# A two-layer decoder trunk on one core: another place for the first tiles of weight chunks, and another order of steps in both mixers

## The chip, the core and the metric

The kernel runs on one core of a Trainium2 chip. Times are microseconds on the device for one execution of the whole program, and a comparison takes the median of several runs. The core has five engines that work side by side, each through its own list of instructions in order: TensorE (PE, with its weight loads shown as PEld), VectorE (DVE), ScalarE (ACT), GpSimd (POOL), and SyncE (SP), which here only issues transfers. They wait for each other by semaphores.

## The reference, cut to what matters

The input is 256 tokens of width 1,024 in float32. Two layers each do this, and a last RMSNorm follows:

```python
for layer in range(2):
    h = h + 0.5 * swiglu(rms_norm(h, ffn1_norm[layer]), w_gate, w_up, w_down)
    h = h + mixer(rms_norm(h, mix_norm[layer]))
    h = h + 0.5 * swiglu(rms_norm(h, ffn2_norm[layer]), w_gate, w_up, w_down)

def swiglu(x, w_gate, w_up, w_down):         # 1024 -> 2816 -> 1024
    return (silu(x @ w_gate) * (x @ w_up)) @ w_down
```

The mixer of layer 0 projects to q, k, v of eight heads of 64 and to u, v of a gating branch. The heads attend over three dilated windows, which the kernel folds into one additive mask. The branch takes gelu of u and v, normalises v, mixes it over positions with a causal 128 x 128 matrix for each of four groups, and multiplies by u. Both parts go through one output projection. The mixer of layer 1 is causal attention with 16 heads of 64; with 256 tokens its blocks come down to the one own block.

## The kernel before, in words

The residual stream is kept turned around in `X`: eight tiles of 128 columns of x by 256 tokens. For each matmul stage `Next` makes two tiles of it, `xTh` (x times the norm's gain, rounded to the short float32 format that TensorE takes) and `xTl` (what the rounding left). The weights are cut in the same way into `whi` and `wlo`. One product is then three matmuls (`mm3`, lines 199 to 202): whi with xTh (line 200), whi with xTl (line 201), wlo with xTh (line 202). The factor 1/rms of the norm is put in when a result is taken out of PSUM (`norm["row"]`, `norm["col"]`).

Weights come as a stream of chunks (`Stream`, line 40) of 2,048 columns per partition, 1 MB each. `load_one` has SP load a chunk into one of three raw buffers. `split_parts` makes whi on ACT (line 87) and wlo on DVE (line 88) out of it, in a few pieces (`cuts`), into one of four buffers each, which have 64 elements (`LINE`) to spare. `take` hands a chunk to PE; `free` gives its buffers back and has the next ones loaded and split. The order of chunks is written out in lines 161 to 182.

A chunk of a 256-wide weight block has eight tiles of 256 columns, one for each tile of x. PE goes through it twice, for the first 128 columns of each tile (j = 0) and for the second (j = 1): 2 x 8 x 3 = 48 matmuls, each with 128 weight columns against 256 columns of xTh or xTl. All tiles stand `SHIFT` = 16 elements past the start of the buffer, and the start is a multiple of 256 bytes, as are those of xTh, xTl and the other moving tiles. In some chunks, those with `reset`, the first two tiles, here called the head of the chunk, stand at 0 in place of 16 (`at`, line 78). In the feed-forward blocks these are the chunks named in `again`: 1 and 3 in the first block, 2 and 3 in the others. In the mixers they are the chunks of columns 1536 and 0 (first) and 0 and 512 (second).

A feed-forward block (`ffn`, line 429) makes 22 chunks of gate and up columns in turn (n = 0 to 21). `sums` and `spread` behind chunks 1 and 2 make the norm's factor; `gated` takes each pair out into hT. Then come the down columns: 12 chunks, 528 matmuls. In the last block the down product is made in rows of tokens instead (`finish`), so x is turned back for it by 16 transposes on PE and four copies on ACT (`turn_back`, line 440), behind chunk n = 2.

In the mixers one tile of 128 output columns after the other is made on PE (24 matmuls each, `tile_of`), and between these the steps of attention are hung in as events at numbered slots (`at`, `run_events`): `scores(h)` (two products for each half of the queries, softmax on DVE and ACT, scaling on ACT in the first mixer and on POOL in the second), `turn(h)` (three transposes and a split), `weighted(p)` (the product with v for two heads), and `mixing(g)` of the gating branch. `put_k` takes a k tile out of PSUM and has POOL copy halves of kh and kl to the other partitions (lines 625 and 626). A slot is one such tile, or one k step of the output projection (`project`): slots 12 to 19 in the first mixer, 20 to 27 in the second. In the first mixer the tiles come as u, u, q, k, q, k by chunk.

The first chunk of the program is special (`begin`, line 346): x comes in rows of tokens, and PE turns it by transposes (line 394), half before part 0 and half before part 2 of the chunk; ACT and DVE make xTh and xTl from PSUM between the pieces of the split. `heat` puts in matmuls without use.

Of the kernel before, what the change touches and what calls it, by code (L numbers as in the profile page):

```python
# [10 lines left out]
F32 = mybir.dt.float32  # L11
F32R = mybir.dt.float32r
# [3 lines left out]
S = 256  # L16
# [9 lines left out]
PATTERNS = ((128, 1), (512, 4), (2048, 16))  # L26

RAW, SPL = 3, 4
PAIRS = 3
HEAT0, HEAT1 = 6, 4  # L30


LINE, SHIFT = 64, 16
EDGE, GAP = 56, 32

RESET = 2
DOWN = ((0, 8), (8, 8), (16, 6))


class Stream:  # L40
# [7 lines left out]
    def add(self, src, nk, w, shift=0, cuts=(), reset=0):  # L48

        loads = 4 if not self.specs else 2 if len(self.specs) < 4 else 1  # L50
        cuts = (reset, 5, nk) if reset else (*(cuts or (nk / 2,)), nk)
        self.specs.append((src, nk, w, loads, shift, cuts, reset))

    def load_one(self, between=lambda i: None):
# [16 lines left out]
    def split_parts(self):  # L71
        j = self.split
        nc = self.nc
        _, nk, w, _, shift, cuts, reset = self.specs[j]
        raw = self.raws.pop(j)
        his, los = (p.tile([128, CH + LINE], F32R, name=m) for p, m in ((self.hi_pool, "whi"), (self.lo_pool, "wlo")))

        def at(k):
            return int(k * w) + (shift if k >= reset else 0)

        self.parts[j] = tuple([t[:, at(k) : at(k) + w] for k in range(nk)] for t in (his, los))
        k0 = 0
        for k1 in cuts:
            a, n = at(k0), int((k1 - k0) * w)
            r = raw[:, int(k0 * w) : int(k0 * w) + n]
            hi, lo = his[:, a : a + n], los[:, a : a + n]
            nc.scalar.activation(hi, r, AF.Copy)  # L87
            nc.vector.tensor_sub(lo, r, hi.bitcast(F32))  # L88
            k0 = k1
            yield  # L90
        self.split += 1
# [25 lines left out]
def trunk(ctx: ExitStack, tc: tile.TileContext, a, out):  # L117
# [18 lines left out]
    def add_cols(m, c0, w, cuts=(), reset=0):  # L136
        n = CH // w
        for k in range(0, KD, n):
            st.add(m[k * 128 : (k + n) * 128, c0 : c0 + w], n, w, SHIFT if w == 256 else 0, cuts, reset)

    def add_ffn(wg, wu, wd, last=False, again=(2, 3)):
        n0 = len(st.specs)
        for c in range(0, FF, 256):
            for m in (wg, wu):
                add_cols(m, c, 256, *((), RESET) if len(st.specs) - n0 in again else (() if st.specs else (2, 4, 6), 0))
        if last:
            for k in range(0, FT, 2):
# [15 lines left out]
    wab = a["ab_w_in"][0]  # L163
    add_cols(wab, 1024, 512)
    add_cols(wab, 2048, 512)
    add_cols(wab, 1536, 256, reset=RESET)
    add_cols(wab, 1792, 256)
    for c in range(2):
        add_cols(wab, c * 256, 256, reset=0 if c else RESET)
        add_cols(wab, 512 + c * 256, 256)  # L170
    add_mix(a["ab_w_out"][0], MIX1)
    add_ffn(a["ffn2_w_gate"][0], a["ffn2_w_up"][0], a["ffn2_w_down"][0])
    add_ffn(a["ffn1_w_gate"][1], a["ffn1_w_up"][1], a["ffn1_w_down"][1])
# [5 lines left out]
        add_cols(wc, c * 256, 256, reset=0 if c % 2 else RESET)  # L179
        add_cols(wc, 1024 + c * 256, 256)  # L180
    add_mix(a["c_w_out"][0], MIX2)
    add_ffn(a["ffn2_w_gate"][1], a["ffn2_w_up"][1], a["ffn2_w_down"][1], True)


    def rows(v, n):
# [160 lines left out]
    def begin(fp):  # L346
# [40 lines left out]
        parts = st.split_parts()  # L387
        p = bank()
        for i in range(4):
            if i % 2 == 0:  # L390
                for t in range(NT):
                    for k in range(2 * i, 2 * i + 4):
                        c = k % 2 * S + t * 128
                        nc.tensor.transpose(px[k // 2][:, c : c + 128], xr[t][:, k * 128 : (k + 1) * 128], ident)
                if i == 0:
                    heat(HEAT1)
            src = both(px[i])
            nxt.hi(2 * i, src[:, 0])
            nxt.lo(2 * i, src[:, 0])
            next(parts)  # L400
            nxt.hi(2 * i + 1, src[:, 1])
            nxt.lo(2 * i + 1, src[:, 1])
            w = st.parts[0]
            for k in (2 * i, 2 * i + 1):
                for j in range(2):
                    cs = slice(j * 128, (j + 1) * 128)
                    mm3(p[:, j * S : (j + 1) * S], w[0][k][:, cs], w[1][k][:, cs], xT["h"][:, k], xT["l"][:, k],
                        k == 0 and j == 0, k == KD - 1 and j == 1)
# [20 lines left out]
    def ffn(phase):  # L429
        nonlocal nxt  # L430
        with tc.tile_pool(name="fp", bufs=1) as fp:
# [28 lines left out]
            for n in range(FT):  # L460
                k, m = n - n % 2, n % 2
                if phase == n == 0:
                    with tc.manual_schedule():
                        p, turn_gains = begin(fp)
                else:
                    p = bank()
                    w = st.take()
                    colwise(p, w, LATE) if n == 0 else colwise(p, w)
                    st.free()
                ready.append(p)  # L470
                if n == 1 and phase:
                    nxt.sums()
                if n == 2:
                    nxt.spread()
                    if last:
                        turn_back()
                    if phase == 0:
                        turn_gains(1)
                        turn_gains(2)
                    gated(0, *ready[:2])  # L480
                elif n > 2 and m == 1:
                    gated(k, *ready[-2:])
# [109 lines left out]
    def make_attention(mp, mask_cols, nheads, v, mix, engine, rows=False):  # L592

        qs, ks, probs, pts = {}, {}, {}, {}
        mask = mp.tile([128, 384], F32, name="mask")
        nc.scalar.dma_start(mask, a["consts"][:, mask_cols])

# [4 lines left out]

        def put_q(p, bk):

            qq = mp.tile([128, 2 * S + LINE], F32R, name="q", bufs=PAIRS)
            t = bk[:, :S] if rows else scaled(bk)
            for j in range(2):
                q = qq[:, SHIFT + j * S : SHIFT + (j + 1) * S]
                r = slice(j * 64, j * 64 + 64)
                o = slice(64 - j * 64, 128 - j * 64)  # L610
                nc.scalar.activation(q[r, :], t[r, :], AF.Copy)
                nc.vector.tensor_sub(q[o, :], t[r, :], q[r, :].bitcast(F32))  # L612
                qs[2 * p + j] = q

        def put_k(p, bk):

            t = scaled(bk)
            for j in range(2):
                kh = mp.tile([128, S], F32R, name=f"kh{j}", bufs=PAIRS)
                kl = mp.tile([128, S], F32R, name=f"kl{j}", bufs=PAIRS)  # L620
                r = slice(j * 64, j * 64 + 64)
                o = slice(64 - j * 64, 128 - j * 64)
                nc.scalar.activation(kh[r, :], t[r, :], AF.Copy)
                nc.vector.tensor_sub(kl[r, :], t[r, :], kh[r, :].bitcast(F32))
                nc.gpsimd.tensor_copy(kh[o, :], kh[r, :].bitcast(F32))  # L625
                nc.gpsimd.tensor_copy(kl[o, :], kl[r, :].bitcast(F32))
                ks[2 * p + j] = (kh, kl)

        def scores(h):
            q = qs.pop(h)  # L630
            kh, kl = ks.pop(h)
            sc = bank()
            pr = mp.tile([128, 384], F32, name="pr", bufs=4)
            nm = wk.tile([128, 2], F32, name="nm")
            l = wk.tile([128, 2], F32, name="l")
            for b in range(2):
# [76 lines left out]
    def ab_mixer(phase):  # L713
        with tc.tile_pool(name="mp", bufs=1) as mp:
# [57 lines left out]
                ev.setdefault(s, []).append(lambda: f(*args))  # L772

            at(0, turn_spatial)
            for i, s in enumerate((2, 4, 5, 6)):
                at(s, mixing, i)
            for h, s in enumerate((7, 8, 9, 10, 12, 12, 13, 13)):
                at(s, scores, h)
            for h, s in enumerate((10, 11, 11, 12, 14, 14, 15, 15)):
                at(s, turn, h)  # L780
            for p, s in enumerate((12, 13, 15, 17)):
                at(s, weighted, p)

            slot = 0
# [1 line left out]
            def tiles(put):  # L786

                nonlocal slot
                w = st.take()
                for j in range(2):  # L790
                    p = bank()
                    tile_of(p, w, j)
                    put(j, p)
                    run_events(ev, slot)
                    slot += 1
                st.free()
# [2 lines left out]
                nc.vector.tensor_mul(uT[:, i, :], p[:, :S], norm["row"])  # L799
                nc.scalar.activation(uT[:, i, :], uT[:, i, :], AF.Gelu_apprx_tanh)  # L800

            for c in range(2):
                tiles(lambda j, p: put_u(2 * c + j, p))
            for c in range(2):
                tiles(lambda j, p: put_q(2 * c + j, p))
                tiles(lambda j, p: put_k(2 * c + j, p))
            project(mix, MIX1, phase, lambda i: run_events(ev, 12 + i))
            assert not ev

# [6 lines left out]
    def c_mixer(phase):  # L816
        with tc.tile_pool(name="mp", bufs=1) as mp:
# [12 lines left out]
                run_events(ev, slot)  # L830
                slot += 1

            for h, s in enumerate((4, 5, 6, 8, 8, 10, 11, 12, 15, 16, 17, 18, 19, 20, 20, 21)):
                at(s, scores, h)
            for h, s in enumerate((6, 7, 8, 10, 11, 12, 13, 14, 17, 18, 19, 20, 22, 22, 22, 23)):
                at(s, turn, h)
            for p, s in enumerate((9, 12, 14, 16, 20, 22, 23, 23)):
                at(s, weighted, p)

            token_block(0, lambda t, p: put_v(v, t, p))  # L840
# [64 lines left out]
```

## Time and profile before

| | us |
|---|---|
| median of three runs | 983.91 |
| lowest, highest | 982.74, 984.88 |
| the profiled execution | 984.41 |
| its span, from first to last instruction | 982.7 |

The profile is of one execution. Its page names for each engine the busy time, the chain of work that ended last, and groups of instructions by line; x and a number is how many there are. Behind a second bar in a group's row stands the idle time of the engine just before these instructions, and who ended it. In rows in order of time the first number is the start, the second the length, and in brackets the idle time before it. Matmuls are pipelined: the next begins before the last one's end, so what a stream of them costs is the distance between starts. TensorE's clock (PEclk) is given as the granted share.

Two lines of the page show the clock over the whole run, and the transfers:

```profile
PEclk9999999999999999999999999999999999999999
DMA  9866555674446556546656655566434465565531
```

In tenths: the clock is full nearly throughout (two stretches of 3.4 us are too short to show in slices of 24.6 us), and the 16 DMA engines are near full load only at the very start.

### The profile page before, as it was taken

The numbers are of one execution on the slowest core, as the hardware profiler recorded it, in microseconds if no ns is written. First come the engines' busy times: TensorE is split into PE (matmuls) and PEld (weight loads), VectorE is DVE, ScalarE is ACT, GpSimd is POOL, SyncE is SP. The second block draws the span as 40 slices with busy tenths as digits, with TensorE's granted clock in tenths as the row PEclk, the third lists the DMA queues.
The fourth block names the chain that finished last, engine by engine and source line by source line (L and its number), as shares of the span: only waits on it lengthen the run. The fifth ranks groups of instructions, "written<-read, shape, count | busy, mean of one in ns | idle before, by whom it ended". The sixth has DMA issues, their size and how long they took to land.

```text
span 982.7 us, 18088 instructions
## 1 busy us (share of the span) xinstructions
PE 964.9 (98%) x7679; PEld 939.4 (96%) x7679; DVE 615.0 (63%) x877; ACT 504.7 (51%) x794; POOL 64.7 (7%) x98
## 2 busy tenths in 40 slices
PE   9999999999999999999999999999999999999997
PEld 8999999989899999999999999999888999999886
DVE  6856556558876655645755665566879776566443
ACT  6644444465885544443544444345767665444431
POOL 0000000001200000000000000000546200000000
PEclk9999999999999999999999999999999999999999
DMA  9866555674446556546656655566434465565531
GB/s 282 277 191 195 164 186 166 215 237 146 129 130 196 190 174 199 176 156 200 202 183 191 195 174 176 180 195 210 148 129 129 129 195 171 181 202 175 191 110 43
DMA packets 153537, 174.86 MB, mean 178 GB/s; under 512 B 3008, under 2 KB 142192, under 8 KB 153456
## 3 DMA queue, kind: packets, MB, share of 16 engines
q1 hardware_dynamic: 151888, 171.54, 54.7%
q10 hardware_dynamic: 1568, 2.17, 0.6%
q8 instruction: 60, 0.98, 0.4%
q14 instruction: 21, 0.17, 0.0%
HBM read 172.65 MB, written 1.05 MB: 177 GB/s over the span
## 4 chain that ended last, share of the span: by engine, by line
PE 86%; ACT 5%; DVE 4%; issue 3%; POOL 1%; POOLq 0%; ACTq 0%
PE bank L201 26%; PE bank L200 26%; PE bank L202 26%; PE bank L518 2%; PE bank L515 2%; PE bank L514 2%; ACT whi L87 2%; DVE wlo L88 2%; ACT pr L645 1%; ACT pr L652 1%; PE bank L662 0%; PE bank L639 0%; DVE q L612 0%; POOL kh L625 0%; ACT pth L205 0%
## 5 line engine op out<-in xcount | busy, mean ns | idle before, releaser
L87 ACT ACTIVATE whi<-raw 128x1024 fp32r<-128x1024 f32 (+2 forms) x344 | 329.5, 1002 | 400.0 <-issue 311.0
L88 DVE TENSOR_TENSOR wlo<-raw,whi 128x1024 fp32r<-128x1024 f32 (+2 forms) x344 | 388.0, 1162 | 140.8 <-ACT whi L87 139.4
L200 PE MATMUL bank<-xTh,whi 128*128 128x256 f32 x1632 | 460.3, 282 | 1.6 <-ACT whi L87 0.9
L201 PE MATMUL bank<-xTl,whi 128*128 128x256 f32 x1632 | 459.0, 281 | 0.5 <-DVE xTl L238 0.5
L202 PE MATMUL bank<-xTh,wlo 128*128 128x256 f32 x1632 | 458.7, 281 | 0.4 <-DVE wlo L88 0.4
L200 PEld LDWEIGHTS bank<-xTh,whi 128*128 128x128 f32 x1632 | 312.8, 192 | 2.1 <-ACT whi L87 1.1
L201 PEld LDWEIGHTS bank<-xTl,whi 128*128 128x128 f32 x1632 | 307.4, 188 | 0.9 <-DVE xTl L238 0.9
L202 PEld LDWEIGHTS bank<-xTh,wlo 128*128 128x128 f32 x1632 | 307.3, 188 | 0.9 <-DVE wlo L88 0.9
L200 PE MATMUL bank<-hTh,whi 128*128 128x256 f32 x528 | 148.4, 281 | 0.0
L202 PE MATMUL bank<-hTh,wlo 128*128 128x256 f32 x528 | 148.4, 281 | 0.0
L201 PE MATMUL bank<-hTl,whi 128*128 128x256 f32 x528 | 148.4, 281 | 0.0
L200 PEld LDWEIGHTS bank<-hTh,whi 128*128 128x128 f32 x528 | 101.4, 192 | 0.0
L201 PEld LDWEIGHTS bank<-hTl,whi 128*128 128x128 f32 x528 | 99.1, 188 | 0.0
L202 PEld LDWEIGHTS bank<-hTh,wlo 128*128 128x128 f32 x528 | 99.1, 188 | 0.0
L457 DVE TENSOR_TENSOR hm<-gs,bank 128x512 f32<-128x512 f32 x44 | 30.1, 686 | 88.8 <-PE bank L202 86.6
L454 DVE TENSOR_TENSOR gs<-bank,row 128x512 f32<-128x512 f32 x44 | 30.0, 689 | 56.4 <-PE bank L202 56.3
L209 POOL TENSOR_TENSOR rstd<-ms,half_neg 128x2 f32<-128x2 f32 x6 | 5.5, 917 | 637.5 <-DVE ms L268 438.5
L201 PE MATMUL bank<-mixl,whi 128*128 128x256 f32 x128 | 35.5, 279 | 0.0
L200 PE MATMUL bank<-mixh,whi 128*128 128x256 f32 x128 | 35.5, 280 | 0.0
L202 PE MATMUL bank<-mixh,wlo 128*128 128x256 f32 x128 | 35.3, 277 | 0.0
L206 DVE TENSOR_TENSOR hTl<-hm,hTh 128x512 fp32r<-128x512 f32 x44 | 30.1, 684 | 2.1 <-ACT hTh L205 2.1
L514 PE MATMUL bank<-whi,hTh 128*128 128x512 f32 x80 | 31.1, 389 | 0.0
(135 smaller groups left out, 864.1 us busy)
## 6 DMA issues: line engine op xcount, KB each, us to landing
raw<-in_ffn_w_gate SPq DMA_DIRECT2D x42, 1024.0 KB, 5.4
raw<-in_ffn_w_up SPq DMA_DIRECT2D x42, 1024.0 KB, 5.3
raw<-in_ffn_w_down SPq DMA_DIRECT2D x35, 1024.0 KB, 5.1
raw<-in_c_w_in SPq DMA_DIRECT2D x12, 1024.0 KB, 5.2
raw<-in_ab_w_in SPq DMA_DIRECT2D x10, 1024.0 KB, 5.2
raw<-in_ffn_w_down SPq DMA_DIRECT2D x12, 768.0 KB, 4.4
raw<-in_ab_w_out SPq DMA_DIRECT2D x4, 1024.0 KB, 5.1
raw<-in_c_w_out SPq DMA_DIRECT2D x4, 1024.0 KB, 4.9
```

The source lines that it names most:

```text
L87: nc.scalar.activation(hi, r, AF.Copy)
L88: nc.vector.tensor_sub(lo, r, hi.bitcast(F32))
L200: nc.tensor.matmul(p, sh, mh, start=start, stop=False)
L201: nc.tensor.matmul(p, sh, ml, start=False, stop=False)
L202: nc.tensor.matmul(p, sl, mh, start=False, stop=stop)
L206: nc.vector.tensor_sub(lo, src, hi.bitcast(F32))
L454: nc.vector.tensor_mul(g, both(pg), twice(norm["row"]))
L457: nc.vector.tensor_mul(hm, g, both(pu))
L514: nc.tensor.matmul(banks[t, h], sh, w[0][kw][:, cs], start=k == 0, stop=False)
L515: nc.tensor.matmul(banks[t, h], sh, w[1][kw][:, cs], start=False, stop=False)
L518: nc.tensor.matmul(banks[t, h], sl, w[0][kw][:, cs], start=False, stop=k == FT - 1)
L645: nc.scalar.activation(pr[:, cs], pr[:, cs], AF.Exp, bias=nm[:, b : b + 1], scale=-1.0, accum_out=l[:, b : b + 1])
```

## The change

Five things are changed.

- *Heads.* A head has three tiles in place of two. They stand behind the other five, at the end of the buffer, and begin 52 elements (208 bytes) past a multiple of 256 bytes, where the old ones were at 0. The other five begin at the buffer's start, shifted by 16 elements as before. The split of such a chunk has two pieces (three tiles and five) in place of three (two, three, three); in the first block three (three, three, two).
- *Which chunks have heads.* As before in the first three feed-forward blocks; the last block has them in chunk 7 too. In the first mixer four chunks have them in place of two.
- *The first mixer's chunks take turns*: u, q, u, k, q, k in place of u, u, q, k, q, k. Mixing, scores, turns and the weighted sums get other slots.
- *In the second mixer* scores and turns of most heads come one to two slots later; k and q get four buffers each in place of three, pr five in place of four.
- *x is turned back* in the last block behind chunk n = 6 in place of n = 2. In `begin` the second half of x is turned before part 1 in place of part 2.

```diff
-RESET = 2
+RESET, RESHIFT = 3, 52
...
-        cuts = (reset, 5, nk) if reset else (*(cuts or (nk / 2,)), nk)
+        cuts = (*((reset,) if reset else ()), *(cuts or (() if reset else (nk / 2,))), nk)
...
-            return int(k * w) + (shift if k >= reset else 0)
+            return int((k - reset) * w) + shift if k >= reset else int((nk - reset + k) * w) + RESHIFT
...
-                add_cols(m, c, 256, *((), RESET) if len(st.specs) - n0 in again else (() if st.specs else (2, 4, 6), 0))
+                add_cols(m, c, 256, *(() if n0 else (6,), RESET) if len(st.specs) - n0 in again else (() if st.specs else (2, 4, 6), 0))
...
-    add_cols(wab, 1536, 256, reset=RESET)
-    add_cols(wab, 1792, 256)
-    for c in range(2):
-        add_cols(wab, c * 256, 256, reset=0 if c else RESET)
-        add_cols(wab, 512 + c * 256, 256)
+    for c in (1536, 0, 1792, 512):
+        add_cols(wab, c, 256, reset=RESET)
+    for c in (256, 768):
+        add_cols(wab, c, 256)
...
-    add_ffn(a["ffn2_w_gate"][1], a["ffn2_w_up"][1], a["ffn2_w_down"][1], True)
+    add_ffn(a["ffn2_w_gate"][1], a["ffn2_w_up"][1], a["ffn2_w_down"][1], True, (2, 3, 7))
...
-            if i % 2 == 0:
+            if i < 2:
                 for t in range(NT):
-                    for k in range(2 * i, 2 * i + 4):
+                    for k in range(4 * i, 4 * i + 4):
...
+                if last and n == 6:
+                    turn_back()
                 if n == 2:
                     nxt.spread()
-                    if last:
-                        turn_back()
...
+        pairs, flying = (4, 5) if rows else (3, 4)
...
-            for i, s in enumerate((2, 4, 5, 6)):
+            for i, s in enumerate((3, 4, 5, 6)):
                 at(s, mixing, i)
-            for h, s in enumerate((7, 8, 9, 10, 12, 12, 13, 13)):
+            for h, s in enumerate((8, 9, 10, 11, 12, 12, 13, 13)):
                 at(s, scores, h)
-            for h, s in enumerate((10, 11, 11, 12, 14, 14, 15, 15)):
+            for h, s in enumerate((11, 11, 12, 13, 14, 14, 15, 15)):
                 at(s, turn, h)
-            for p, s in enumerate((12, 13, 15, 17)):
+            for p, s in enumerate((12, 14, 15, 16)):
                 at(s, weighted, p)
...
-            for c in range(2):
-                tiles(lambda j, p: put_u(2 * c + j, p))
-            for c in range(2):
-                tiles(lambda j, p: put_q(2 * c + j, p))
-                tiles(lambda j, p: put_k(2 * c + j, p))
+            for put, c in ((put_u, 0), (put_q, 0), (put_u, 1), (put_k, 0), (put_q, 1), (put_k, 1)):
+                tiles(lambda j, p: put(2 * c + j, p))
...
-            for h, s in enumerate((4, 5, 6, 8, 8, 10, 11, 12, 15, 16, 17, 18, 19, 20, 20, 21)):
+            for h, s in enumerate((5, 6, 7, 8, 9, 10, 11, 12, 16, 16, 17, 18, 20, 20, 21, 21)):
                 at(s, scores, h)
-            for h, s in enumerate((6, 7, 8, 10, 11, 12, 13, 14, 17, 18, 19, 20, 22, 22, 22, 23)):
+            for h, s in enumerate((8, 9, 10, 11, 12, 13, 14, 15, 19, 19, 20, 20, 22, 22, 23, 23)):
                 at(s, turn, h)
-            for p, s in enumerate((9, 12, 14, 16, 20, 22, 23, 23)):
+            for p, s in enumerate((10, 12, 14, 16, 20, 22, 23, 24)):
                 at(s, weighted, p)
```

More of the change, by code (lines that the diff above doesn't have):

```diff
@@ L28 @@
 RAW, SPL = 3, 4
-PAIRS = 3
 HEAT0, HEAT1 = 6, 4
@@ L603, in put_q @@
         def put_q(p, bk):
-            qq = mp.tile([128, 2 * S + LINE], F32R, name="q", bufs=PAIRS)
+            qq = mp.tile([128, 2 * S + LINE], F32R, name="q", bufs=pairs)
             t = bk[:, :S] if rows else scaled(bk)
@@ L618, in put_k @@
             for j in range(2):
-                kh = mp.tile([128, S], F32R, name=f"kh{j}", bufs=PAIRS)
-                kl = mp.tile([128, S], F32R, name=f"kl{j}", bufs=PAIRS)
+                kh = mp.tile([128, S], F32R, name=f"kh{j}", bufs=pairs)
+                kl = mp.tile([128, S], F32R, name=f"kl{j}", bufs=pairs)
                 r = slice(j * 64, j * 64 + 64)
@@ L632, in scores @@
             sc = bank()
-            pr = mp.tile([128, 384], F32, name="pr", bufs=4)
+            pr = mp.tile([128, 384], F32, name="pr", bufs=flying)
             nm = wk.tile([128, 2], F32, name="nm")
```

## The prediction

> **What bounds the kernel now.** I read the page first (busy shares, clock, chain), then the groups by shape, then windows and single rows to get the spacing of matmuls, and last the waits of PE.
>
> ```profile
> span 982.7 us, 18088 instructions
> PE 964.9 (98%) x7679; PEld 939.4 (96%) x7679; DVE 615.0 (63%) x877; ACT 504.7 (51%) x794; POOL 64.7 (7%) x98
> PE 86%; ACT 5%; DVE 4%; issue 3%; POOL 1%; POOLq 0%; ACTq 0%
> ```
>
> TensorE sets the end: 98% busy, 86% of the chain. So only two things can move the time: the spacing of matmuls that follow each other without a wait, and the waits of PE. Spacing first. A matmul's own duration (0.28 us) overlaps the next, so spacing is read from starts.
>
> ```profile
> L200 PE MATMUL bank<-xTh,whi 128*128 128x256 f32 x1632 | 460.3, 282 | 1.6 <-ACT whi L87 0.9 <-ACT half L288 0.7
> L201 PE MATMUL bank<-hTl,whi 128*128 128x256 f32 x528 | 148.4, 281 | 0.0
> L201 PE MATMUL bank<-mixl,whi 128*128 128x256 f32 x128 | 35.5, 279 | 0.0
> ```
>
> There are 3 x 1,632 + 3 x 528 + 3 x 128 = 6,864 matmuls of 256 columns. Windows give how many fall in a stretch (those that only reach into it are counted too, so the spacing is about the stretch plus 0.28, divided by the count):
>
> ```profile
> core 0: us, PE busy (x), PEclk, DMA share, GB/s
> 60.00:160.00 100.00, 100.00 (x852) 1.00 0.58 182
> 301.10:306.10 5.00, 5.00 (x47) 1.00 0.69 206
> 248.40:251.80 3.40, 3.40 (x18) 0.51 0.33 130
> 712.70:716.10 3.40, 3.17 (x9) 0.51 0.45 113
> ```
>
> 100.28 / 852 = 0.1177 us in the first feed-forward block. The stretch at 301 is faster, at the same clock and for the same instructions. Its exact spacing, and a place where it changes, by first and last rows:
>
> ```profile
> 15.58 0.28 PE L200 MATMUL bank<-xTh,whi 128*128 128x256 f32 x1
> 15.94 0.28 PE L200 MATMUL bank<-xTh,whi 128*128 128x256 f32 x1
> ...
> 28.59 0.28 PE L200 MATMUL bank<-xTh,whi 128*128 128x256 f32 x1
> 30.17 0.28 PE L202 MATMUL bank<-xTh,wlo 128*128 128x256 f32 x1
> 30.29 0.28 PE L200 MATMUL bank<-xTh,whi 128*128 128x256 f32 x1
> 31.00 0.28 PE L200 MATMUL bank<-xTh,whi 128*128 128x256 f32 x1
> 31.59 0.28 PE L202 MATMUL bank<-xTh,wlo 128*128 128x256 f32 x1
> ...
> 301.22 0.28 PE L200 MATMUL bank<-xTh,whi 128*128 128x256 f32 x1
> 306.09 0.28 PE L201 MATMUL bank<-xTl,whi 128*128 128x256 f32 x1
> ```
>
> From 301.22 to 306.09 lie 43 spacings (14 triples and one): 4.87 / 43 = 0.1133. From 28.59 to 30.17, 14 spacings: 0.113. Then at 30.29 the second half of the same chunk begins with its two head tiles (six matmuls, to 31.00: 0.118 each), and behind them the tail stays at 0.59 / 5 = 0.118. The head matmuls from 15.58 to 15.94 take 0.36 / 3 = 0.120. So there are **two spacings for one instruction, 0.1133 and 0.1177, each of which keeps itself up**, and heads at offset 0 threw PE from the fast into the slow one. In the groups the fast stretch (from 301.1 to 305.9) shows up in the mean duration:
>
> ```profile
> L201 PE MATMUL bank<-xTl,whi 128*128 128x256 f32 x15 | 4.1, 276 | 0.0
> ```
>
> 276 ns here, 281 or 282 over all, 279 in the projections behind the mixers, so the four feed-forward blocks ran slow almost throughout.
>
> **The change part by part.** (1) *Heads.* Per full block 22 chunks x 48 + 528 down matmuls = 1,584; with the last block's 1,056 that makes 5,808 in the four blocks. At 0.1177 - 0.1133 = 0.0044 us each, all of them fast is worth 25.6 us. The three new head tiles begin 36 elements past the end of the five tail tiles, at offset 52 elements where the old ones had 0. The trace has no matmul at this offset, so its effect is bounded from both sides. Best: every block is fast from chunk 2 on. Off go chunks 0 and 1 of three blocks (6 x 48 x 0.0044 = 1.3 us) and the heads themselves: 15 chunks have them (2 + 4 + 2 + 2 + 2 + 3), 15 x 18 = 270 matmuls, by the nearest rows 0.120, 270 x 0.0067 = 1.8 us. Net 25.6 - 3.1 = 22.5 us off. Worst: the tails take over the heads' 0.120, 5,808 x 0.0023 = 13.4 us more. I take the best end, less 0.5 for chunks switched back by steps in between (the moved turn-back, ahead of the new heads in chunk 7): **-22**; the mixers, partly fast already, are left at 0. My reason is the 30.29 row: the state is switched by what a head does to the stream, the old heads switched it the wrong way in the second half of a chunk, and with any head that does not do so the runs at 28.59 and 301.22 would have gone on. That 0.1133 holds through a block without waits is an inference; these rows show it for 5 us.
>
> The Trainium skill ("SBUF — State Buffer", section "Who interferes with whom") gives PE two independent read ports and says that PE never waits on anyone, which would leave offsets in SBUF without effect. By that rule term (1) is 0. The trace does not agree: it has two spacings at one clock, and rows where heads change them. The rule still makes a rival of its own (C below).
>
> (2) *Waits of PE*, all of them:
>
> ```profile
> PE bank L662 <- POOL pr L654: 2.6, 2, 2.1
> PE bank L638 <- POOL kh L625: 2.1, 2, 1.5
> PE bank L639 <- POOL kl L626: 1.7, 3, 0.7
> PE bank L200 <- ACT whi L87: 0.9, 1, 0.9
> PE bank L200 <- ACT half L288: 0.7, 1, 0.7
> PE bank L760 <- DVE vn L750: 0.7, 1, 0.7
> ```
>
> *First mixer.* Scores of head 0 stand in slot 7, right behind the tile that follows k's first tile:
>
> ```profile
> 245.24 0.28 PE L202 MATMUL bank<-xTh,wlo 128*128 128x256 f32 x1
> 246.39 1.11 POOL L625 CAST kh<-kh 64x256 fp32r<-64x256 f32 x2 [17.21 <-ACT kh L623]
> 247.02 0.38 PE L638 MATMUL bank<-kh,q 128*128 128x256 f32 x1 [1.50 <-POOL kh L625]
> 248.09 0.39 PE L639 MATMUL bank<-kl,q 128*128 128x256 f32 x1 [0.69 <-POOL kl L626]
> ```
>
> Scores need POOL's copies. From 245.24 to the second product at 248.09 pass 2.85 us instead of 0.23, so 2.6 us are lost, and the pause drops the clock: in 248.40:251.80 it is 0.51, half of 3.4 us, 1.7 lost (18 matmuls where 30 fit bears that out, less the part that would have been switch time; I take 1.5). In the new order k's first chunk stays in slots 6 and 7, while scores move to slots 8, 9, 10, 11: one tile more, 24 x 0.1133 = 2.7 us, against 2.85 needed. Left over: 0.1 to 0.3. The mixing of group 0 goes from slot 2 to 3, another 2.7 us over a wait of
>
> ```profile
> 229.62 0.49 PE L760 MATMUL bank<-wsT,vn 128*128 128x128 f32 x2 [0.68 <-DVE vn L750]
> ```
>
> 0.68 and 0.2 of restart, as at 245.24 (2.6 lost for 1.50 + 0.69 of waiting): 0.9 us, which goes. Together 2.6 + 1.5 + 0.9 - 0.3 = **-4.7**. Queued behind the moved steps on ACT and DVE are the splits of the next chunks; PE waits for none of these in this mixer, and four split buffers stand ahead.
>
> *Second mixer.* Turns wait for POOL's scaling:
>
> ```profile
> 709.69 0.28 PE L639 MATMUL bank<-kl,q 128*128 128x256 f32 x1
> 712.03 0.33 PE L662 MATMUL bank<-ident,pr 128*128 128x128 f32 x1 [2.06 <-POOL pr L654]
> 712.93 0.69 PE L662 MATMUL bank<-ident,pr 128*128 128x128 f32 x2 [0.57 <-POOL pr L654]
> ```
>
> 709.69 to 712.93 loses 3.0 us, and the clock at 712.70 is again 0.51: 1.5 more. The new slots give each head three slots from scores to turn in the first half in place of two or three, and scores two slots from k in place of one, which removes the other kh and kl waits: (2.1 - 1.5) + (1.7 - 0.7) = 1.6, with three restarts of 0.2 as above 2.2. In all 6.7; I take **-6**, as turns and weighted sums now crowd into slots 19 to 24 and POOL's queue is the same length. The fourth k/q buffer and the fifth pr buffer cover heads that now stay in flight longer.
>
> (3) *Start.* The second four columns of x are turned ahead of part 1 in place of part 2:
>
> ```profile
> 2.68 0.94 SPq L355 DMA_DIRECT2D xr<-in_x  x2
> DMA to landing us min/median/max: 2.6/4.4/5.5
> 10.27 1.04 PE L394 MATMUL bank<-ident,xr 128*128 128x128 f32 x8
> 12.17 0.39 PE L200 MATMUL bank<-xTh,whi 128*128 128x256 f32 x1 [0.86 <-ACT whi L87]
> ```
>
> PE waited 0.86 us while ACT first cast what had just been turned. Turned 12 matmuls (1.4 us) earlier, ACT's work lies under part 1: **-0.9**, if x is there: the last half issues by 3.2 and lands by 3.2 + 5.5 = 8.7, when part 0 ends at about 8.9 (10.27 less part 1's twelve matmuls of 0.1133). If it lands later, PE waits for it; the range takes in that nothing is gained here.
>
> (4) *Turn-back at n = 6.*
>
> ```profile
> 808.57 0.39 PE L200 MATMUL bank<-xTh,whi 128*128 128x256 f32 x1 [0.69 <-ACT half L288]
> ```
>
> The 16 transposes stay; at n = 2 they pushed ACT's work for this chunk out by 0.7 us, at n = 6 the splits are chunks ahead and ACT's four copies lie under a chunk of 5.4 us: **-0.7**; if the cover is gone the same 0.7 comes back.
>
> (5) *Cuts.* Two pieces of 768 and 1,280 columns in place of 512, 768, 768; DVE and ACT (63% and 51% busy) do this chunks ahead: 0. No DMA is added; SP's loads keep their order except for the first mixer's chunks, taken in the new order.
>
> Sum against the profiled run (984.4 us, span 982.7 and 1.7 around it; the median is 983.9): 984.4 - 22 - 4.7 - 6 - 0.9 - 0.7 = **950**. Waits alone give -12.3, bounds -7 (half of the two mixers' terms fails, start fails) to -14.
>
> **The rivals.** *B, heads hold in part*: fast in two of the blocks, or until something switches back. For it: the fast run from 28.59 lasted half a chunk only, and the last block turns x in between. Half of 22: 984.4 - 11 - 12.3 = 961. *C, heads do nothing to the state*: the offset does not matter, or each tail falls back into the slow spacing as at 31.00. 984.4 - 12.3 + 1 for the wider heads = 973. Against it: heads did switch at 30.29. The rule of the Trainium skill named above would give this case. *D, slower*: the offset of 52 locks the tails into the heads' spacing or one beyond it. The first step, 0.120, costs 13.4 in the blocks and 2.4 in the mixers (1,056 x 0.0023), 15.8 against 12.3 of waits: 988; it decides from a spacing of about 0.1195 on. For it: 0.120 is seen, at another offset; against it: at 31.00 a tail leaves its head's 0.120 at once.
>
> **How the numbers follow.** A 0.47, B 0.22, C 0.20, D 0.11. The predicted time is A's, 950. A's own range is 943 to 956; B fills 955 to 967, C 968 to 977. From 941 to 980 takes in A, B and C with their unknowns; it leaves out most of D and about 0.05 to 0.08 for a sum outside its bounds. 0.2% is about 2 us, what these runs can tell from no change. Faster by more: A, B, C and a little of D, 0.88; same 0.03; slower 0.09.
>
> **What would show it.** Right: mean durations of L201 and L202 in the blocks near 276 to 278 in place of 281, some 885 matmuls per 100 us in place of 852 (100.28 / 0.1133), no clock of 0.5 between 200 and 790 us, PE's waits on POOL under 1.5 us in all. Wrong in (1): 852 per 100 us as before (C), or a count that changes between blocks (B), or about 836 (D). Wrong in (2): new waits of PE on POOL or ACT, above all in slots 19 to 24 of the second mixer. What would break the whole prediction is a third spacing at offset 52.

## The result, and the profile after

The changed kernel takes **978.65 us** (median of five runs, 977.56 to 980.35) against 983.91 (982.74 to 984.88): a ratio of 0.9948 with a 95% interval of 0.9934 to 0.9963. It is faster, by 5 us; 34 were forecast. The profiled execution takes 977.56, with this head of the page:

```profile
span 975.8 us, 18069 instructions
PE 960.6 (98%) x7679; PEld 935.7 (96%) x7679; DVE 614.5 (63%) x867; ACT 504.4 (52%) x784; POOL 68.4 (7%) x98
PE 84%; DVE 6%; ACT 5%; issue 3%; POOL 1%; DMA 1%; POOLq 0%; SPq 0%; ACTq 0%; DVEq 0%
```

PE still sets the end. Its busy time fell by only 4.3 us (964.9 to 960.6), where 22 was to come out of its spacing. In the chain of waits DVE has 6% in place of 4%: waits have changed hands. The windows with PE alone (stretch, its length, busy time and count of matmuls, granted clock, DMA) show the spacing in the four feed-forward blocks:

```profile
core 0: us, PE busy (x), PEclk, DMA share, GB/s
60.00:160.00 100.00, 100.00 (x852) 1.00 0.57 182
340.00:440.00 100.00, 100.00 (x851) 1.00 0.55 179
520.00:620.00 100.00, 100.00 (x851) 1.00 0.58 185
830.00:900.00 70.00, 70.00 (x597) 1.00 0.58 184
```

852, 851, 851 per 100 us, and 70.28 / 597 = 0.1177: all four blocks run at the slow spacing, the first at exactly the count of before. Where the 6.9 us of span came from is seen by stage. The borders are the first matmul of each stage in the trace, so a wait at a border counts to the stage ahead of it (us, one trace each; the heads of the columns are explained below):

| stage | before | after | once | four | old heads | old heads, early turn-back |
|---|---|---|---|---|---|---|
| start and block 1 | 197.1 | 196.3 | 190.0 | 189.9 | 196.0 | 195.7 |
| first mixer | 97.8 | 97.8 | 99.4 | 97.9 | 97.9 | 99.4 |
| block 2 | 187.3 | 186.8 | 180.7 | 181.1 | 187.5 | 187.5 |
| block 3 | 187.3 | 187.0 | 180.8 | 180.4 | 187.3 | 187.3 |
| second mixer | 118.4 | 114.9 | 114.2 | 115.2 | 115.1 | 114.9 |
| block 4 and finish | 194.8 | 192.9 | 189.6 | 189.7 | 190.5 | 194.7 |
| span | 982.7 | 975.8 | 954.7 | 954.2 | 974.3 | 979.4 |

So the blocks in the middle gave 0.8 us together, the first mixer nothing, the second mixer 3.5, start 0.8, the last block 1.9. One program's first mixer differs by some 1.5 us from one execution to the next: *old heads* and its variant with early turn-back have the same one, at 97.9 and 99.4. Smaller differences there show nothing.

**What the new heads did.** Chunk 2 of block 2 in the timeline of the changed kernel (start, duration, engine, line). At 306.64 PE is in the tail of the first pass (j = 0), at 308.34 the head of the second pass (j = 1) begins, at 309.39 its tail:

```profile
306.64 0.28 PE L198 MATMUL bank<-xTh,whi 128*128 128x256 f32 x1
...
308.34 0.28 PE L198 MATMUL bank<-xTh,whi 128*128 128x256 f32 x1
309.39 0.28 PE L198 MATMUL bank<-xTh,whi 128*128 128x256 f32 x1
...
310.81 0.28 PE L198 MATMUL bank<-xTh,whi 128*128 128x256 f32 x1
```

Before the head: 15 spacings in 1.70 us, 0.1133. Through the head: nine in 1.05, 0.1167. Behind it: 12 in 1.42, 0.1183, and it stays there. The head at offset 52 took PE **from fast to slow**. The first pass of the same chunk had come out fast, right after other work of PE. Counted over all 30 head passes of this trace, by the spacing of the tail ahead and behind: of the ten that followed a fast tail without a break, ten came out slow; of the two that followed a slow tail without a break, two came out fast; of the 18 with other work or a wait of PE ahead of them or among their first matmuls (a break of the stream, in what follows), 17 came out fast. The traces of the runs below that have heads of three tiles add 28 of 28 from fast to slow and six of six from slow to fast (the first pass of chunk 1 in block 1, close to the start, left out: in two of them the stream breaks a few matmuls behind its head). An unbroken pass turns the spacing over, and each chunk is passed twice: what the first pass puts right the second undoes.

The last block shows it in two windows. Behind the turned heads of chunk 3 it ran fast until chunk 7's heads:

```profile
806.50:822.50 16.00, 16.00 (x144) 1.00 0.61 188
826.50:900.00 73.50, 73.50 (x627) 1.00 0.59 186
```

16.28 / 144 = 0.113 for chunks 4 to 6, 73.78 / 627 = 0.1177 behind the second pass of chunk 7.

**What became of the waits.** The waits of PE in the changed kernel (engine, line, who ended the wait: us in all, times, longest):

```profile
PE bank L661 <- DVE ptl L204: 2.5, 2, 1.5
PE bank L661 <- ACT pr L651: 1.6, 1, 1.6
...
PE bank L198 <- DVE nm L641: 1.0, 2, 0.8
PE bank L198 <- ACT whi L86: 0.7, 1, 0.7
...
PE bank L638 <- POOL kl L625: 0.3, 1, 0.3
PE bank L392 <- DMA xr<-in_x: 0.2, 1, 0.2
```

The 6.4 us of waits for POOL are down to 0.3, as planned. In their place the turns of probabilities (L661) wait for ACT's scaling and for DVE's copies. Two of these stand in the first mixer. Behind the first of them the granted clock falls to a half again; behind the second, nearly as long, it does not (rows of the timeline, then windows):

```profile
258.81 0.83 PE L661 MATMUL bank<-ident,pr 128*128 128x128 f32 x3 [1.58 <-ACT pr L651]
266.42 0.55 PE L661 MATMUL bank<-ident,pr 128*128 128x128 f32 x3 [1.51 <-DVE ptl L204]
```
```profile
core 0: us, PE busy (x) PEld busy (x) DVE busy (x) ACT busy (x) POOL busy (x), PEclk, DMA share, GB/s
252.00:256.00 4.00, 4.00 (x38) 4.00 (x37) 2.78 (x13) 3.94 (x10) 0.00 (x0) 1.00 0.83 254
256.00:260.00 4.00, 2.35 (x19) 1.92 (x19) 2.59 (x8) 3.95 (x10) 0.00 (x0) 1.00 0.03 8
260.00:264.00 4.00, 4.00 (x23) 4.00 (x23) 3.80 (x10) 3.92 (x12) 2.64 (x5) 0.57 0.29 78
```

1.58 and 1.51 with 0.2 of restart each, and 23 matmuls from 260 to 264 where 35 fit (12 x 0.1133 = 1.4), make 4.9 us; the old waits with their clock were put at 5.0. ACT is busy 3.92 to 3.95 us of each 4 around it.

### The profile page after: what moved, and what is told of

It reads as the page before. It is cut to its first block, busy times and chain, and to the rows that moved or that the text cites. A ratio compares the mean times of both kernels' runs of the same rounds, so it can differ in the third digit from the quotient of the medians.

```text
span 975.8 us, 18069 instructions
## 1 busy us (share of the span) xinstructions
PE 960.6 (98%) x7679; PEld 935.7 (96%) x7679; DVE 614.5 (63%) x867; ACT 504.4 (52%) x784; POOL 68.4 (7%) x98
## 3 DMA queue, kind: packets, MB, share of 16 engines
HBM read 172.65 MB, written 1.05 MB: 178 GB/s over the span
## 4 chain that ended last, share of the span: by engine, by line
PE 84%; DVE 6%; ACT 5%; issue 3%; POOL 1%; DMA 1%; POOLq 0%; SPq 0%; ACTq 0%; DVEq 0%
PE bank L198 26%; PE bank L199 26%; PE bank L200 26%; DVE wlo L87 3%; ACT whi L86 2%; PE bank L516 2%; PE bank L513 2%; PE bank L512 2%; ACT pr L644 1%; DMA raw<-in_ffn_w_gate 1%; DVE ptl L204 1%; DVE kl L623 0%; ACT pr L651 0%; DVE q L611 0%; DVE pr L641 0%
## 5 line engine op out<-in xcount | busy, mean ns | idle before, releaser
L200 PEld LDWEIGHTS bank<-xTh,wlo 128*128 128x128 f32 x1632 | 311.7, 191 | 0.8 <-DVE wlo L87 0.6
L198 PEld LDWEIGHTS bank<-xTh,whi 128*128 128x128 f32 x1632 | 306.4, 188 | 1.0 <-ACT whi L86 0.9
L200 PEld LDWEIGHTS bank<-hTh,wlo 128*128 128x128 f32 x528 | 101.4, 192 | 0.0
L198 PEld LDWEIGHTS bank<-hTh,whi 128*128 128x128 f32 x528 | 99.1, 188 | 0.0
L653 POOL TENSOR_SCALAR pr<-pr,rl 128x128 f32<-128x128 f32 (+1 forms) x32 | 30.2, 958 | 21.0 <-DVE rl L647 15.0
```

What stands on the lines that cost most here:

```text
L198: nc.tensor.matmul(p, sh, mh, start=start, stop=False)
L200: nc.tensor.matmul(p, sl, mh, start=False, stop=stop)
L653: engine.tensor_scalar(pr[:, cs], pr[:, cs], rl[:, b : b + 1], None, op0=ALU.mult)
```

## The experiments

Theory T: a pass of a three-tile head at offset 52 that follows tails unbroken turns the spacing over; with two passes in each chunk the blocks end slow. Rival U: the fast spacing is not there for the taking in long blocks, or heads are not what sets it. For the rest, whether steps moved in the mixers lose their waits or hand them on.

**Once**: heads at 52 for the first pass alone, in the same chunks; the columns of the second pass stand at 16 like the tail.

```diff
-RESET, RESHIFT = 3, 52
+RESET = (3, 52, (0,))
...
+        def half(t, j):
+            b = (nk - reset) * w + (reset * 128 + off if j in passes else shift)
+            return t[:, b : b + reset * 128]
```

> The changed kernel with one difference: the three head tiles stand at offset 52 for the first pass of a chunk (first 128 columns) only; for the second pass they stand like the tail. Theory T (each pass over a head at 52 turns the spacing over, fast to slow and slow to fast, or sets it fast right behind a restart; a chunk makes two passes, so the second undoes the first): from chunk 3 on the blocks run at 0.1133, about 885 matmuls per 100 us, and the time falls from 978.7 to 950 to 962. Rival U (the fast spacing dies by itself within half a chunk, whatever the second head does): 977 to 980, 852 per 100 us.

Measured: 956.37 (955.07 to 956.90), 0.9717 of the kernel before (0.9702 to 0.9731). The same windows of PE:

```profile
60.00:160.00 100.00, 100.00 (x884) 1.00 0.59 190
340.00:440.00 100.00, 100.00 (x885) 1.00 0.60 191
520.00:620.00 100.00, 100.00 (x885) 1.00 0.60 192
```

100.28 / 885 = 0.1133: the fast spacing holds through whole blocks. U falls. All that PE sees differently from the changed kernel is the second pass, and it is worth 978.65 - 956.37 = 22.3 us. (The head is also made in two halves, one more instruction on ACT and one on DVE in each of these chunks.)

**None**: no heads in the four blocks (the mixers keep theirs).

```diff
-    ... again=(1, 3))
+    ... again={})
...
```

> The changed kernel without heads in the four feed-forward blocks (those of the mixers stay). T: each block keeps, from chunk 3 to its end, the one spacing that the last restart of PE left, so every block is uniform, 0.1133 or 0.1177, and the time is 955 to 980 by how many are fast. U: all slow, 978 to 980. A third view (heads are needed to reach the fast spacing at all): all blocks slow from chunk 3 on, 979.

Measured: 964.87 (964.53 to 965.43), 0.9805 (0.9789 to 0.9822). The blocks differ, each uniform:

```profile
60.00:160.00 100.00, 100.00 (x851) 1.00 0.58 182
340.00:440.00 100.00, 100.00 (x884) 1.00 0.60 191
520.00:620.00 100.00, 100.00 (x885) 1.00 0.61 191
```

Block 1 is slow, blocks 2 and 3 fast: without heads a block keeps what the last break left. Block 4 was not uniform: chunks 3 to 6 ran fast, and behind the turned-back x it was slow (chunk 6 at 0.1135, chunk 7 at 0.1179), so a break can also leave PE slow. No heads at all beat the change by 14 us. By the rule of the Trainium skill as the prediction read it ("SBUF — State Buffer", section "Who interferes with whom", on the ports that engines share), that PE never waits on anyone, leaving heads out would have done nothing; the counts here say otherwise.

**Middle**: heads added in the middle of blocks, where no other step of PE is near: three tiles for one pass in chunks 8 and 14 of block 1, for both passes in block 2; in block 3 two tiles, then four, for one pass; in block 4 three tiles at 52 for one pass, then two at the old offset for both.

```diff
+    ... again={1: RESET, 3: RESET, 8: ONCE, 14: ONCE})
+    ... again={2: RESET, 3: RESET, 8: RESET, 14: RESET})
+    ... again={2: RESET, 3: RESET, 8: (2, 52, (0,)), 14: (4, 52, (0,))})
+    ... True, {2: RESET, 3: RESET, 10: ONCE, 15: (2, 64, (0, 1))})
```

> The changed kernel with more heads in the middle of undisturbed, slow stretches. First block: chunks 8 and 14, first pass only. Second: chunks 8 and 14, both passes. Third: chunk 8 two tiles, chunk 14 four tiles, first pass only. Last block: chunk 10 three tiles, first pass only, chunk 15 two tiles at offset 64 (the same as 0 to 256 bytes), both passes; none in chunk 7. T: block 1 fast from chunk 8 to 14 and slow behind; block 2 fast for the 39 matmuls between the two heads of a chunk and slow behind; last block slow from chunk 15 on at the latest; about 975 to 978. U: the spacing behind a lone head falls back within half a chunk in block 1. Third view (heads work only behind a restart): no change of spacing at 8 and 14.

Measured: 970.64 in one run. Windows of PE between these heads:

```profile
32.00:54.00 22.00, 22.00 (x189) 1.00 0.77 237
58.00:86.00 28.00, 28.00 (x250) 1.00 0.61 188
92.00:120.00 28.00, 28.00 (x240) 1.00 0.59 179
342.00:371.00 29.00, 29.00 (x249) 1.00 0.58 182
...
530.00:556.00 26.00, 26.00 (x232) 1.00 0.64 202
562.00:600.00 38.00, 38.00 (x338) 1.00 0.59 189
```

22.28 / 189 = 0.1179, 28.28 / 250 = 0.1131, 28.28 / 240 = 0.1178: one pass turns slow to fast at chunk 8, holds for six chunks, and one pass turns it back at chunk 14. Behind both passes (342) all is slow as ahead of them. Two tiles at 52 also turned slow to fast (530). Four tiles did not turn fast to slow: the stretch behind them (562) stays at 38.28 / 338 = 0.1133. In block 4 chunk 10 took the stream from fast to slow, and the two old tiles of chunk 15 left it slow. The expectation gave no outcome for block 3; fast from chunk 8 to its end, it took 181.8 us where the changed kernel takes 187.0, and that is enough to bring the total under the 975 to 978 expected.

**Old heads**: the changed kernel with the two-tile heads at 0 and their chunks as before; slots, start and late turn-back new.

```diff
-RESET, RESHIFT = 3, 52
+RESET = 2
...
-            return int((k - reset) * w) + shift if k >= reset else int((nk - reset + k) * w) + RESHIFT
+            return int(k * w) + (shift if k >= reset else 0)
...
-    ... True, (2, 3, 7))
+    ... True)
```

> The changed kernel with the heads of before (two tiles at 0, in the chunks and pieces of before; the order of chunks, slots, start and turn-back as changed). If the waits gave most of the gain: 979.5 to 981.5. If the new heads gave most of it: 982.5 to 984.

Measured: 976.6 (976.04 to 978.0), 0.9926 (0.9911 to 0.9942). Below both expectations: everything but the new heads gives some 7 us (984.8 x 0.0074), no less than the whole change. The last block explains most of it, 190.5 against 194.8 in the kernel before, with this window:

```profile
830.00:900.00 70.00, 70.00 (x620) 1.00 0.61 194
```

70.28 / 620 = 0.1134 where the changed kernel has 597: the last block is fast here. Two runs looked for the cause.

**No chunk 7**: the changed kernel without chunk 7's heads.

```diff
-    ... True, (2, 3, 7))
+    ... True)
```

> The changed kernel with one thing undone: chunk 7 of the last block has no heads (chunks 2 and 3 keep theirs). Theory T (a head pass at offset 52 that follows tails without a break turns the spacing over, so the second of chunk 7's two passes is what ended the fast stretch 806.5 to 822.5): the last block stays fast from chunk 4 on, 15 chunks x 48 x 0.0044 = 3.2 us less in it (192.9 -> 189.7), total 978.65 - 3.2 = 975.4, and the window behind 826.5 holds some 650 matmuls per 73.5 us in place of 627. Rival U (the fast spacing dies out by itself, or the turned-back x ends it): 978 to 979, 627 per 73.5 us as before.

Measured: 972.2, with four runs from 968.57 to 977.51; ratio 0.9885 (0.9843 to 0.9927). In the profiled execution (977.51) the window holds 620 and the last block takes 190.5, 2.4 less than in the changed kernel:

```profile
830.00:900.00 70.00, 70.00 (x620) 1.00 0.59 192
```

So chunk 7's second pass is what ended the fast stretch: x is turned back here too, and the block stays fast to its end. It gained 2.4 and not the 3.2 expected because chunks 4 to 6 were slow in this execution: chunk 3's first pass had come out fast behind a break, so its second left the stream slow, and the turned-back x brought it back. The total of that execution is no better, since its first mixer took 99.2 and its start 0.6 more. Two other runs are 8 to 9 us lower, somewhat more than a whole block at the fast spacing saves (1,584 x 0.0044 = 7.0); they left no trace, and what they did differently stays open. One program can thus come out differently from run to run.

**Early turn-back**: the kernel with old heads and x turned back at n = 2 again.

```diff
-                if last and n == 6:
-                    turn_back()
                 if n == 2:
                     nxt.spread()
+                    if last:
+                        turn_back()
```

> The kernel with the old heads and the new slots (976.6), with x turned back at n = 2 again in place of n = 6. Theory T (in that kernel the 16 transposes at n = 6 broke the stream behind the last head and PE came back in the fast spacing, which then held to the end of the last block): without that break the last block is slow again, 190.5 -> some 194.5, total 980.5 to 981.5. Rival W (the late turn-back is worth only the wait of 0.7 us that it removes, and the fast spacing has another cause): 977.0 to 977.6.

Measured: 981.59 (979.94 to 982.53), 0.9975 (0.9965 to 0.9985), with 597 in the window and 194.7 in the last block:

```profile
830.00:900.00 70.00, 70.00 (x597) 1.00 0.58 183
```

Moving 16 transposes by four chunks is worth 5.0 us with the old heads by the medians, 4.2 in the stage. Only 0.7 of it is the wait. The rest is that at n = 6 they break the stream behind the last head, and PE came back fast (in *old heads* chunk 6 runs at 0.1177, chunk 7 at 0.1132). What a break leaves is not fixed by the step that breaks: in *none* the same 16 transposes left a fast stream slow.

**Four**: the changed kernel with heads of four tiles, both passes.

```diff
-RESET, RESHIFT = 3, 52
+RESET, RESHIFT = 4, 52
```

> The changed kernel with heads of four tiles in place of three (all else as it is, both passes over each chunk keep the head). Theory F4 (four tiles leave the fast spacing fast, as at 557.66 in the run with heads in the middle of blocks, and also bring a slow one to fast): blocks fast from chunk 2 on, 181 us for each of the middle blocks, total 954 to 960. Rival P (a head pass turns the spacing over whatever its width, and 557.66 was chance): blocks slow as in the changed kernel, 977 to 980. In between, 962 to 972, if four tiles keep fast what is fast but do not free the slow: then each block follows what its interruptions leave.

Measured: 957.11 (955.90 to 957.41), 0.9725 (0.9710 to 0.9739). All blocks fast:

```profile
60.00:160.00 100.00, 100.00 (x885) 1.00 0.59 190
340.00:440.00 100.00, 100.00 (x884) 1.00 0.59 188
520.00:620.00 100.00, 100.00 (x885) 1.00 0.59 189
```

An unbroken pass over a head of four tiles leaves PE fast whatever came before: in this trace 11 of 11 behind a fast tail, and the one behind a slow tail; the two traces with scaling on POOL below add four of four behind a slow one. The one here is in chunk 2 of block 3, whose first pass, after a break, had come out slow (tail of the first pass from 481.65, head of the second from 483.06, its tail from 484.47):

```profile
481.65 0.28 PE L198 MATMUL bank<-xTh,whi 128*128 128x256 f32 x1
...
483.06 0.28 PE L198 MATMUL bank<-xTh,whi 128*128 128x256 f32 x1
484.47 0.28 PE L198 MATMUL bank<-xTh,whi 128*128 128x256 f32 x1
485.83 0.38 PE L282 MATMUL bank<-ident,wide 128*128 128x128 f32 x2
```

1.41 / 12 = 0.1175 ahead of the head and through it, 1.36 / 12 = 0.1133 behind it.

**Slots**: *once*, with the first mixer's turns of heads 1 and 2 a slot later.

```diff
-            for h, s in enumerate((11, 11, 12, 13, 14, 14, 15, 15)):
+            for h, s in enumerate((11, 12, 13, 13, 14, 14, 15, 15)):
                 at(s, turn, h)
-            for p, s in enumerate((12, 14, 15, 16)):
+            for p, s in enumerate((13, 14, 15, 16)):
                 at(s, weighted, p)
```

> The kernel with heads for the first pass alone (956.37), with the first mixer's turns of heads 1 and 2 one slot later (turns in slots 11, 12, 13, 13, 14, 14, 15, 15; weighted sums in 13, 14, 15, 16). Theory S (the moved slots let turns come before ACT's scaling and DVE's copies are done): the waits of 1.6 (ACT pr) and 2.1 us (DVE ptl) and the stretch at half clock behind them go, 3 to 5 us less in the first mixer, total 951.5 to 953.5. Rival Q (DVE and ACT are behind by as much there whatever the slot): the waits turn up one slot later, 955.5 to 957.

Measured: 956.29 (955.33 to 963.05), 0.9734 (0.9700 to 0.9768); first mixer 99.3, as in *once* (99.4). One of the four runs, 963.05, lies about one slow block (7.0 us) above the others; it left no trace. Waits of PE:

```profile
PE bank L682 <- DVE ptl L225: 4.1, 2, 2.6
PE bank L658 <- POOL kh L645: 1.7, 1, 1.7
PE bank L659 <- POOL kl L646: 1.2, 2, 0.7
```

The wait for ACT's scaling is gone, and POOL's copies, gone in the changed kernel, are back with 1.7. Rival Q's time holds: a later slot hands the wait on.

**Scaling on POOL**: *four*, with the first mixer's scaling of pr moved from ACT to POOL; and the same with the later slots of the run before.

```diff
-            ... make_attention(mp, slice(0, 384), 8, v, mix, nc.scalar)
+            ... make_attention(mp, slice(0, 384), 8, v, mix, nc.gpsimd)
```

> The kernel with heads of four tiles (957.1), with the first mixer's scaling of pr (16 instructions of some 0.45 us) on POOL in place of ACT, as the second mixer has it. Theory A (ACT, 3.92 to 4.00 of 4 us busy in four of the five stretches from 252 to 272, is what ends the first mixer; its waits only change their names when slots are moved): 16 x 0.40 = 6.4 us less on ACT, part of them on the path, so the stage of the first mixer goes from 98.0 to 95 to 97 and the total to 954 to 956. Rival G (POOL takes 0.6 to 2.0 us for one such scaling and hands the delay to the same turns): stage 98 or more, total 957 to 960, waits of turns on POOL.

> As the one with the scaling on POOL, and the first mixer's turns of heads 1 and 2 one slot later (turns in 11, 12, 13, 13, 14, 14, 15, 15; weighted sums in 13, 14, 15, 16). Theory A with POOL's longer scaling given the time that it needs: stage of the first mixer 94 to 96, total 952.5 to 955. Rival G: no better than the run without the moved slots, 957 to 960.

Measured: 956.5 (954.77 to 956.64), 0.9712 (0.9685 to 0.9738), and with later slots 954.9 (954.72 to 955.83), 0.9703 (0.9682 to 0.9724); first mixer 99.0 and 97.4. In the first of them ACT is relieved, but DVE takes its place (windows with PE, PEld, DVE, ACT, POOL):

```profile
252.00:256.00 4.00, 2.52 (x21) 2.35 (x21) 3.94 (x9) 2.43 (x7) 2.96 (x5) 1.00 0.14 34
256.00:260.00 4.00, 2.10 (x15) 1.76 (x15) 3.94 (x13) 3.95 (x12) 2.90 (x4) 1.00 0.67 231
```

ACT falls to 2.43 of 4 in the first stretch, DVE is at 3.94 in both, and PE waits as before. So ACT alone is not the bound. Theory A falls without the slots (stage 99.0 where 95 to 97 was expected); with them the total lies in its 952.5 to 955, but the stage, 97.4, missed its 94 to 96. The first mixer took 97.4 to 99.4 us in every version that was tried, and 1.5 of that is what one program varies by. Which work of the three engines would have to go to shorten it stays open. The last version is the quickest of all, 29 us under the kernel before; over *four* alone its gain of 2 us is within the intervals.

## Why the prediction was wrong

**The step that failed is the choice of the best end in (1)**, with its reason that "with any head that does not do so the runs at 28.59 and 301.22 would have gone on". Three inferences in that part were right: two spacings that keep themselves up, heads that switch them, and 0.1133 through a whole block if nothing disturbs it. The size was right too: -22, and the second pass alone measures 22.3 (*once*), four tiles 21.5 (*four*). What was wrong is the new head. It was taken as harmless because it was not at 0. It is no less a switch than the old one: three tiles at 52 take a fast stream to slow in ten passes of ten. The rows at 30.29 held the warning: there the second pass of a chunk undid the first, and the change keeps two passes per chunk. The prediction bounded the effect "from both sides" only by what the tails would settle at, never by a head that switches at each pass. So term (1), -22, came out at next to nothing: the two blocks in the middle gained 0.8 us together, and in the last block chunk 7's heads cost 2.4 us (192.9 with them, 190.5 without).

**(2), first mixer, -4.7: came to 0.** The waits named did go (scores and mixing), but the turns now wait for ACT's scaling and DVE's copies, 4.9 us with restarts and clock against the old 5.0. The prediction called the steps queued behind the moved ones splits that PE does not wait for, and put new waits of turns at nothing. It did not look at how full ACT is. In the kernel before (columns as in the windows above):

```profile
256.00:260.00 4.00, 4.00 (x39) 4.00 (x37) 3.46 (x10) 3.95 (x12) 0.00 (x0) 1.00 0.87 259
260.00:264.00 4.00, 4.00 (x37) 4.00 (x36) 3.60 (x11) 3.95 (x13) 1.54 (x4) 1.00 0.10 18
```

ACT is as full there as in the changed kernel, and yet PE does not wait. A likely reading is that the old waits gave ACT and DVE the time that they need for this work, and that PE, which now comes to it earlier, waits for the same work later. No run isolates that. Three placements of the same steps, in the changed kernel, *slots* and *scaling on POOL*, each lost a wait and found another.

**(2), second mixer, -6: -3.5.** The mechanism was right: POOL's waits and the stretch at half clock are gone. The allowance of 0.7 for crowding in slots 19 to 24 was too small. There, a turn and a weighted sum wait for DVE, 2.1 us with two restarts of 0.2, where 0.7 was allowed; the other 1.1 us of the shortfall was not traced:

```profile
754.59 1.07 PE L661 MATMUL bank<-ident,pr 128*128 128x128 f32 x6 [0.95 <-DVE ptl L204]
757.14 0.47 PE L198 MATMUL bank<-pth,vth 128*128 128x512 f32 x1 [0.78 <-DVE nm L641]
```

**(3), start, -0.9: -0.8** over the first stage; chunk 1 begins at 14.63 where it began at 15.58. **(5), cuts, 0:** nothing in the trace speaks against it.

**(4), turn-back, -0.7:** the wait went (no wait for ACT's `half` in the list). The step was mis-sized because its effect on the spacing was only seen as a cost ("chunks switched back by steps in between"). With the old heads it is worth 5.0 us (*old heads* against *early turn-back*); in the changed kernel the heads of chunk 7, the very next chunk, took the stream to slow again.

The total of 978.65 stands nearest to rival C (973), but by chance: C had heads do nothing to the state, and here they act on it, twice over, so that the end is slow as before. The gain of the change is that of its slots, start and turn-back. The runs with old heads show them: 0.9975 of before without the late turn-back, 0.9926 with it. The new heads added nothing to that (0.9948).

## What to carry to other kernels

Before a state that switches is priced, count how often the stream passes the switch and ask for the outcome of each pass from each state; "not the bad setting" is not the good setting. Where a tight PE stream shows two spacings at one clock, compare windows of equal length by their counts, and try width and place of the disturbing tiles: here one constant, 3 or 4 tiles, is worth 2.2%. When waits of PE are removed in a stretch where another engine is busy almost without a pause (ACT 3.92 to 3.95 us of each 4 here), allow for their return under another name; here they did so in each placement that was tried, though that the full engine is the reason is argued and not shown.

## What was not expected of the hardware

The spacing of identical matmuls, each with its own weight load, depends on what was passed long before: 0.1133 or 0.1177 us through a block of more than 1,500 matmuls, set by at most 72 matmuls at another address and by what breaks the stream. In an unbroken pass, twelve head matmuls (four tiles) leave the fast spacing from either state, nine (three tiles, at 52 as well) turn it over, and six at the old offset leave the slow one (ten of eleven such passes in the kernel before; the tail behind the other, in chunk 1 of the first block, is at 0.1164 on average). Behind a break the passes over new heads mostly, not always, came out fast (17 of 18 in the changed kernel). What in TensorE holds the state was not tried.
